# The last two chunks of an output product run block by block, with the routing steps written between them, and the first gathered rows in memory of their own

## The chip, the cores and the metric

The kernel runs on one core of one Trainium2 chip. The time is device microseconds of that core. Its engines are TensorE (PE, with weight loads shown as PEld), VectorE (DVE), ScalarE (ACT), GpSimd (POOL) and the queues that issue transfers (SP's and ACT's above all). TensorE's clock has two levels, 1.2 and 2.4 GHz; the profile gives it as a share of the higher one (0.50 or 1.00).

## The reference, cut to what matters

Two transformer layers on 512 tokens of width 1024, in float32. The change touches the passage from the second mixer to the mixture of experts of the second layer:

```
x = x + merged @ w_out[i]                     # the output product
h = rms_norm_2(x, ffn_norm_g[i])
g_sel = argmax(softmax(h @ w_rg + b_rg))      # one of 4 groups
e_in_group = (h @ w_re + b_re)[g_sel]         # 8 experts of the group
top_p, top_i = top_k(softmax(e_in_group), 2)
for each expert e of 32:                      # gate, up and down matrices
    y += combine[:, e] * (silu(h @ w_gate[e]) * (h @ w_up[e])) @ w_down[e]
x = x + y
```

## The kernel before

All matmuls of the product are made in three parts (`mm3`, lines 249 to 251): each float32 operand is a high and a low half, and high by high, high by low and low by high are summed. A weight chunk of 128x1024 is fetched into a tile `wr` (512 KB, SP's queue, L215), ACT rounds it into `wh` (L203) and DVE takes the rest into `wl` (L206). `c.base` has two `wr` and three pairs `wh`, `wl`.

**The output product.** `merged @ w_out` has four column chunks of 256 (n = 0 to 3), each with two weight chunks (k-blocks 0 to 3 and 4 to 7), so eight weight pairs pass through three pair buffers. Tokens come in four blocks of 128 (t). For n = 0 and 1, `proj_b` runs all blocks of one chunk. For n = 2 and 3, `proj_bt` is written block by block: block t with n = 2, then with n = 3, then `routing.block(t)`. It asks for four pairs at once where there are three; the fourth pair (n = 3, k-blocks 4 to 7) takes the buffer of n = 2's first pair once that is done with all four blocks. Outside of hand-written stretches a scheduler orders each engine's instructions ahead of the run, by program order among those that it takes to be ready, so that the order on the engines is not the written one.

**Routing.** `routing.block(t)`: square of the row `x[t]` with its sum (L1278, ACT), eight transposes of `x[t]` into PSUM in two groups of four (L347) and copies to `hT` (L1283), eight float32 matmuls with the 40 router columns (L1286; the trace has two records for each). `route` and `slots` then work on DVE: inverse root of the mean square (`rsqrt`, L323 to L336), logits (L1298), two rounds of "largest and its index" (L1325 to L1344), then a small matmul that ranks the tokens within each expert (L1349, L1350) and the slot number (L1353 to L1361). Blocks 0 and 1 go together, 2 and 3 singly. `xn` and `hf` hold the scaled rows, whole for blocks 2 and 3 and as halves for 0 and 1. PSUM has four `acc` and four `aux` tiles.

**Experts.** `experts` makes from the slots a one-hot matrix `ohq` for 4 experts x 64 slots (L1378, L1379), and TensorE gathers the tokens' rows by multiplying with it (L1391 with halves, L1388 with the whole rows of blocks 2 and 3). The gathered rows are scaled into `xg` (L1493 DVE, L1491 ACT). Then 16 pairs of experts follow: `up` (L1102), two parts of the next gather, `turn`, `down` (L1122). The order on TensorE in this loop is the written one (`manual_schedule`).

**Expert weights.** 192 chunks of 512 KB (L1077, SP's queue) go through 28 buffers: 15 `wc` of `ring2`, 5 of `ring3`, and the 8 of `c.base`. The first 28 can be fetched before the first expert runs; each later one waits for the release of an earlier one. `ring3` stands where the product's operand `xt` was. `rp` (tag `route`) holds the routing's small tiles, and the pool `exp` (with `xg`, `hid`, `hT`, `ye`) stands partly in its place: the first write to `xg` waits until everything in `rp` has been read, the last reader being the routing weights `wt` (L1434).

Of the kernel before, what the change touches and what calls it, by code (L numbers as in the profile page):

```python
# [9 lines left out]
F32 = mybir.dt.float32  # L10
# [31 lines left out]
RING3 = 5  # L42
# [128 lines left out]
class Chip:  # L171
# [146 lines left out]
    def rsqrt(self, ss, scale, tag="rs", pool=None):  # L318

        v = self.nc.vector  # L320
        sh = list(ss.shape)
        ms = self.sm(sh, F32, tag + "m", pool=pool)
        v.tensor_scalar(ms, ss, scale, EPS, op0=OP.mult, op1=OP.add)  # L323
        y = self.sm(sh, F32, tag + "y", pool=pool)
        t = self.sm(sh, F32, tag + "t", pool=pool)
        v.tensor_scalar(t.bitcast(I32), ms.bitcast(I32), 1, None, op0=OP.logical_shift_right)
        v.tensor_scalar(y.bitcast(I32), t.bitcast(I32), -1.0, float(0x5F3759DF), op0=OP.mult, op1=OP.add)

        for k in (1.0, -2.0, 16.0):
            if sh == [128, 1]:  # L330
                v.scalar_tensor_tensor(t, y, y, ms, op0=OP.mult, op1=OP.mult)
            else:
                v.tensor_tensor(t, y, y, op=OP.mult)
                v.tensor_tensor(t, t, ms, op=OP.mult)
            v.scalar_tensor_tensor(y, t, -3.0 * k * k, y, op0=OP.add, op1=OP.mult)
        v.tensor_scalar(y, y, -1.0 / 8192, None, op0=OP.mult)  # L336
        return y
# [449 lines left out]
def second_mixer(c, x, xt, xtp, xpool, extra):  # L787
# [269 lines left out]
    add_product(c, x, xt, lambda n: a["wout2"][n], routing.block)  # L1057
# [23 lines left out]
class Pair:  # L1081
# [4 lines left out]
    def __init__(self, c, p, chunks, wgu, wdn):  # L1086
# [4 lines left out]
        self.rows = p.tile([64 * self.n, D], F32, name=c.name("ye"), tag="ye", bufs=2)  # L1091
# [82 lines left out]
def more_rounds(c, p, ring, x, hf, rel, wt, iota, wgu, wdn, rounds):  # L1174
# [5 lines left out]
    with tc.For_i(0, rounds * N_EXP * SLOTS, N_EXP * SLOTS) as r:  # L1180
        with tc.For_i(0, N_EXP, 1) as e:
# [23 lines left out]
            ex = Pair(c, p, chunks, [wgu[rows]], [wdn[rows]])  # L1205
# [28 lines left out]
class Routing:  # L1234


    def __init__(self, c, x):
# [20 lines left out]
        self.pl, self.rs, self.xn, self.ss = {}, {}, {}, self.sm([NT], "rss")  # L1258
# [15 lines left out]
    def block(self, t):  # L1274
        c, x, rp = self.c, self.x[t], self.rp
        nc, s = c.nc, c.nc.scalar
        hT = rp.tile([128, KB, 128], F32, name=c.name("hT"), tag="hT", bufs=2)
        s.activation(self.hf[t][:, 0], x, AF.Square, accum_out=self.ss[:, t:t + 1])  # L1278
        for q in range(0, KB, 4):
            ps = c.aux()  # L1280
            for j in range(4):
                c.transpose(ps[:, j * 128:j * 128 + 128], x[:, (q + j) * 128:(q + j + 1) * 128])
            (c.nc.vector.tensor_copy if t == NT - 1 and q else s.copy)(hT[:, q:q + 4], ps.rearrange("p (j t) -> p j t", j=4))  # L1283
        self.pl[t] = c.aux()[:, :40]
        for kb in range(KB):
            nc.tensor.matmul(self.pl[t], hT[:, kb], self.wr[:, kb], start=kb == 0, stop=kb == KB - 1)  # L1286
        if t:
            self.route(range(2) if t == 1 else range(t, t + 1))

        s.dma_start(self.xd[t], x)  # L1290

    def route(self, ts):

        c, v, s = self.c, self.c.nc.vector, self.c.nc.scalar
        tt = slice(ts[0], ts[-1] + 1)
        rs = c.rsqrt(self.ss[:, tt], 1.0 / D, f"rr{ts[0]}", self.rp)
        for i, t in enumerate(ts):
            v.scalar_tensor_tensor(self.lg[:, t].rearrange("p g e -> p (g e)"), self.pl[t], rs[:, i:i + 1], self.rb,  # L1298
                                   op0=OP.mult, op1=OP.add)
        for i, t in enumerate(ts):  # L1300
            self.rs[t] = rs[:, i:i + 1]
            if t < SPLIT:
                self.halve(t)
            else:
                self.xn[t] = self.rp.tile([128, D], F32, name=c.name("xn"), tag="xn", bufs=NT - SPLIT)
                s.activation(self.xn[t], self.x[t], AF.Copy, scale=self.rs[t])
        self.slots(ts)

    def halve(self, t):

        x, h, rs = self.x[t], self.hf[t], self.rs[t]
        self.c.nc.scalar.activation(h[:, 0], x, AF.Copy, scale=rs)
        self.c.nc.vector.scalar_tensor_tensor(h[:, 1], x, rs, h[:, 0].bitcast(F32), op0=OP.mult, op1=OP.subtract)

    def slots(self, ts):

        c, n, tt = self.c, len(ts), slice(ts[0], ts[-1] + 1)
        sm, oh = lambda shape, tag, dt=F32: self.sm([n] + shape, f"{tag}{n}", dt), self.oh[:, :, tt]
        v, pe = c.nc.vector, c.nc.tensor
# [24 lines left out]
        v.tensor_tensor(self.both[:, tt], oh[:, 0], oh[:, 1], op=OP.add)  # L1344

        ps = c.aux()[:, :n * 32].rearrange("p (t e) -> p t e", t=n)
# [4 lines left out]
        tmp = [self.sm([2, n, 32], f"rtmp{k}{n}") for k in range(2)]  # L1351
        ee, rk, ri = (self.sm([2, n], f"{k}{n}", dt) for k, dt in (("ree", F32), ("rrk", F32), ("rri", I32)))
        v.tensor_tensor(tmp[0], oh, eidx[:, None, None, :].to_broadcast([128, 2, n, 32]), op=OP.mult)  # L1353
        v.tensor_reduce(ee, tmp[0], axis=AX.X, op=OP.add)
        v.tensor_tensor(tmp[1], ps[:, None].to_broadcast([128, 2, n, 32]), oh, op=OP.mult)
        v.tensor_reduce(rk, tmp[1], axis=AX.X, op=OP.add)
        v.tensor_copy(ri, rk)
        slot = self.slot[:, :, tt]
        v.scalar_tensor_tensor(slot, ee, float(SLOTS), rk, op0=OP.mult, op1=OP.add)
        v.tensor_scalar(ri, ri, 6, None, op0=OP.logical_shift_right)  # L1360
        v.scalar_tensor_tensor(slot, ri, float((N_EXP - 1) * SLOTS), slot, op0=OP.mult, op1=OP.add)  # L1361


def experts(c, x, routing, xtp, pled, out):
# [34 lines left out]
    for t in range(NT):  # L1399
        eq = onehot(oq, t, slot)  # L1400
# [6 lines left out]

    later = ExitStack()
    later.enter_context(tc.issue_after(eq.ins))
    for t in whole:  # L1410
        routing.halve(t)


    sm, (m1, m2) = routing.sm, routing.m
    pr5 = sm([NT, 5, 8], "pr5")
    v.tensor_tensor(pr5, routing.lg, m1[:, :, :, None].to_broadcast([128, NT, 5, 8]), op=OP.subtract)
    s.activation(pr5, pr5, AF.Exp)
    p1, p2 = sm([NT, 5], "p1"), sm([NT, 5], "p2")
    v.tensor_reduce(p1, pr5, axis=AX.X, op=OP.add)
    v.reciprocal(p1, p1)  # L1420
    v.tensor_tensor(p2, m2, m1, op=OP.subtract)
    s.activation(p2, p2, AF.Exp)
    v.tensor_tensor(p2, p2, p1, op=OP.mult)
    sel, pk = sm([2, NT, 4], "sel"), sm([2, NT], "pk")
    for k, m in enumerate((p1, p2)):
        v.tensor_tensor(sel[:, k], m[:, :, 1:], routing.o[0][:, :, 0, 0:4], op=OP.mult)
    v.tensor_reduce(pk, sel, axis=AX.X, op=OP.add)
    den = sm([NT], "rden")
    v.tensor_tensor(den, pk[:, 0], pk[:, 1], op=OP.add)
    v.reciprocal(den, den)  # L1430
    v.tensor_tensor(den, den, p1[:, :, 0], op=OP.mult)
    wt = c.small.tile([128, 2, NT], F32, name="wt", bufs=1)
    sloti = c.small.tile([128, 2, NT], I32, name="sloti", bufs=1)
    v.tensor_tensor(wt, pk, den[:, None, :].to_broadcast([128, 2, NT]), op=OP.mult)  # L1434
    later.close()

    pc = c.aux()
    for t in range(NT):
        pe.matmul(pc[:, :32], routing.onesb, both[:, t], start=t == 0, stop=t == NT - 1)
    cmax = sm([1], "rcmax")  # L1440
    v.tensor_reduce(cmax, pc[:, :32], axis=AX.X, op=OP.max)
    v.tensor_scalar(cmax, cmax, float(SLOTS - 1), None, op0=OP.add)
    extra = p.tile([128, 2], I32, name="extra")
    v.tensor_copy(extra[:, 0:1], cmax)
    v.tensor_scalar(extra[:, 0:1], extra[:, 0:1], 6, None, op0=OP.logical_shift_right)
    v.tensor_scalar(extra[:, 0:1], extra[:, 0:1], -1, None, op0=OP.add)
    v.tensor_scalar(extra[:, 1:2], extra[:, 0:1], 1, None, op0=OP.min)
    rp.release()
    c.dbg("slot", slot)
    c.dbg("wt", wt)  # L1450

    rows = COMBINED * SLOTS
    ydram = c.dram.tile([rows, D], F32, name="ydram")
    first = c.small.tile([128, 2, NT], F32, name="first", bufs=1)
    v.tensor_scalar(first, slot, float(rows), None, op0=OP.is_lt)
    v.tensor_tensor(first, first, wt, op=OP.mult)
    v.tensor_scalar(sloti, slot, float(rows - 1), None, op0=OP.min)

    ring3 = tc.alloc_tile_pool(name="ring3", bufs=1)
    moe, p = p, tc.alloc_tile_pool(name="exp", bufs=1)  # L1460
# [11 lines left out]
    def xg_tile():  # L1472
        return p.tile([128, KB, 4, 64], F32, name=c.name("xg"), tag="xg", bufs=2)

    def onehots(q):
# [4 lines left out]
        return oq, xg_tile()  # L1480

    def dispatch(oq, xg, kb, ps=None):
# [4 lines left out]
        for j in range(2):  # L1487

            xk, pk, g = xg[:, kb + j], ps[:, j].rearrange("p (e n) -> p e n", e=4), c.col("n_ffn2", kb + j)
            if j:  # L1490
                s.activation(xk, pk, AF.Copy, scale=g)  # L1491
            else:
                v.tensor_scalar(xk, pk, g, None, op0=OP.mult)  # L1493
# [16 lines left out]
    def tail():  # L1510
# [56 lines left out]
        def eat(ps, t, o, n=512, eng=None):  # L1567
            ns = slice(o, o + n)
            tag = "ye" if t % 2 else "xg"
            g = p.tile([128, n], F32, name=c.name("g"), tag=tag, bufs=2)  # L1570
# [53 lines left out]
    cur = oq, xg_tile()  # L1624
    for kb in range(0, KB, 2):
        dispatch(*cur, kb, parts[kb // 2])
    with tc.manual_schedule(engines={mybir.EngineType.PE}):
        for e in range(0, N_EXP, 2):
            q, e4 = divmod(e, 4)
            if e4 == 0 and q < 7:  # L1630
                nxt = onehots(q + 1)
            last = Pair(c, p, chunks, [a["wgu"][e + i] for i in range(2)], [a["wdn"][e + i] for i in range(2)])
# [24 lines left out]
    p.release()  # L1657
    ring3.release()
    op.release()
# [129 lines left out]
```

## Time and profile before

| | |
|---|---|
| median of 3 runs | 1644.61 us (1643.86 to 1648.22) |
| the profiled execution, its own time | 1644.96 us |
| its span, first to last instruction | 1643.0 us |
| TensorE busy | 1543.5 us (94%) |
| VectorE busy | 924.6 us (56%) |
| ScalarE busy | 666.6 us (41%) |
| mean granted clock | 0.98 |
| read from memory | 227.00 MB |

The 1.96 us between the span and the execution's time lie outside the first and last instruction. A busy TensorE is not one at its peak, since its matmuls overlap: one is recorded for 0.28 us where the next starts 0.12 us later.

### The profile page before, as it was taken

To read this page: it belongs to the slowest core of one execution; us is meant where nothing else is said; L and a number is where in the kernel's file an instruction comes from. 1 tells how busy PE (TensorE), PEld (TensorE's weight loads), DVE (VectorE), ACT (ScalarE), POOL (GpSimd) and SP (SyncE) were. 2 spreads that over 40 slices of the span, in tenths; PEclk is the share of its full clock that TensorE was granted. 3 is DMA by queue.
4 is the path that set the end of the run, shared out by engine and by line. 5 is a ranking of instruction groups with operands and counts; after the bars stand their busy time and mean duration, and the time that the engine had idled before them with its cause. 6 is when DMAs were issued, how large, how long until landed. Compare 5 with 4: busy or idle time off the path is not lost.

```text
span 1643.0 us, 24293 instructions
## 1 busy us (share of the span) xinstructions
PE 1543.5 (94%) x9602; PEld 1266.7 (77%) x9602; DVE 924.6 (56%) x2109; ACT 666.6 (41%) x1098; POOL 109.3 (7%) x80
## 2 busy tenths in 40 slices
PE   6979899999999999999999997999998899999867
PEld 6757889899899888988899987977888645544356
DVE  4569688878846764265636228777543523221274
ACT  4455546766723543144423334598122211101043
POOL 1052310000000000000000003000000000000042
PEclk9999999999999999999999998999999899999979
DMA  4432122223333322243324332212248499999951
GB/s 158 144 102 84 59 78 78 73 71 115 106 101 116 116 87 71 74 144 100 87 93 167 104 103 90 91 39 90 68 164 295 172 378 371 377 371 379 373 223 54
DMA packets 75466, 244.99 MB, mean 149 GB/s; under 512 B 7728, under 2 KB 16688, under 8 KB 75216
## 3 DMA queue, kind: packets, MB, share of 16 engines
q1 hardware_dynamic: 69152, 220.80, 39.4%
q10 hardware_dynamic: 4464, 16.25, 2.5%
q0 software_dynamic: 1728, 6.29, 1.0%
q8 instruction: 79, 1.29, 0.3%
q14 instruction: 43, 0.35, 0.1%
HBM read 227.00 MB, written 16.32 MB: 148 GB/s over the span
## 4 chain that ended last, share of the span: by engine, by line
PE 67%; DVE 14%; DMA 8%; ACT 6%; issue 3%; POOL 1%; SPq 0%; ACTq 0%; DVEq 0%; POOLq 0%
PE acc L249 16%; PE acc L250 16%; PE acc L251 16%; DMA wc<-in_wgu_dram 5%; PE acc L1102 4%; PE aux L347 3%; PE acc L1122 2%; PE aux L1391 2%; DVE wl L206 2%; ACT wh L203 1%; PE aux L627 1%; DMA ydram<-ye 1%; DVE de L547 1%; ACT pb L604 1%; DVE xn L355 1%
## 5 line engine op out<-in xcount | busy, mean ns | idle before, releaser
L206 DVE TENSOR_TENSOR wl<-wr,wh 128x1024 fp32r<-128x1024 f32 (+1 forms) x178 | 214.8, 1209 | 254.0 <-ACT wh L203 245.5
L203 ACT ACTIVATE wh<-wr 128x1024 fp32r<-128x1024 f32 (+1 forms) x182 | 189.5, 1046 | 318.1 <-PE acc L251 165.6
L250 PE MATMUL acc<-xtl,wh 128*128 128x512 f32 (+2 forms) x744 | 278.7, 375 | 0.0
L249 PE MATMUL acc<-xth,wh 128*128 128x512 f32 (+2 forms) x744 | 277.4, 373 | 1.3 <-ACT wh L203 1.2
L251 PE MATMUL acc<-xth,wl 128*128 128x512 f32 (+2 forms) x744 | 276.8, 372 | 0.0
L249 PE MATMUL acc<-wh,xth 128*128 128x256 f32 x928 | 262.9, 284 | 3.3 <-ACT z L408 1.8
L250 PE MATMUL acc<-wl,xth 128*128 128x256 f32 x928 | 262.4, 283 | 3.2 <-DVE wl L206 1.8
L251 PE MATMUL acc<-wh,xtl 128*128 128x256 f32 x928 | 263.7, 285 | 0.8 <-DVE xtl L206 0.8
L249 PEld LDWEIGHTS acc<-wh,xth 128*128 128x128 f32 x928 | 176.0, 190 | 7.9 <-ACT z L408 3.5
L250 PEld LDWEIGHTS acc<-wl,xth 128*128 128x128 f32 x928 | 176.2, 190 | 5.3 <-DVE wl L206 3.0
L251 PEld LDWEIGHTS acc<-wh,xtl 128*128 128x128 f32 x928 | 176.3, 190 | 1.9 <-DVE xtl L206 1.0
L249 PEld LDWEIGHTS acc<-xth,wh 128*128 128x128 f32 (+1 forms) x744 | 139.4, 187 | 27.2 <-ACT wh L203 1.9
L251 PEld LDWEIGHTS acc<-xth,wl 128*128 128x128 f32 (+1 forms) x744 | 139.3, 187 | 25.2 <-issue 0.5
L250 PEld LDWEIGHTS acc<-xtl,wh 128*128 128x128 f32 (+1 forms) x744 | 139.3, 187 | 24.1 <-issue 0.5
L1102 PE MATMUL acc<-wc,xg 128*64 128x512 f32 x512 | 130.5, 609 | 11.6 <-DMA wc<-in_wgu_dram 6.4
L1102 PEld LDWEIGHTS acc<-wc,xg 128*64 128x64 f32 x512 | 40.7, 139 | 98.2 <-issue 65.3
L249 PE MATMUL acc<-wh,acth 128*128 128x256 f32 x352 | 98.7, 280 | 0.1
L251 PE MATMUL acc<-wh,actl 128*128 128x256 f32 x352 | 98.3, 280 | 0.0
L250 PE MATMUL acc<-wl,acth 128*128 128x256 f32 x352 | 98.2, 279 | 0.0
L1106 DVE TENSOR_TENSOR hid<-hid,acc 128x256 f32<-128x256 f32 x16 | 6.7, 421 | 116.4 <-ACT hid L1105 116.3
L249 PEld LDWEIGHTS acc<-wh,acth 128*128 128x128 f32 x352 | 66.5, 189 | 0.6 <-ACT acth L203 0.5
L761 DVE SCALAR_TENSOR_TENSOR fcv<-acc,cols,fcv 128x511 f32<-128x511 f32 x88 | 65.7, 747 | 1.5
(452 smaller groups left out, 2636.4 us busy)
## 6 DMA issues: line engine op xcount, KB each, us to landing
wc<-in_wgu_dram SPq DMA_DIRECT2D x128, 512.0 KB, 9.3
wc<-in_wdn_dram SPq DMA_DIRECT2D x64, 512.0 KB, 10.1
wr<-in_wup_dram SPq DMA_DIRECT2D x44, 512.0 KB, 3.6
wr<-in_w2a_dram SPq DMA_DIRECT2D x28, 512.0 KB, 3.5
wr<-in_wqkv_dram SPq DMA_DIRECT2D x24, 512.0 KB, 3.7
wr<-in_wout_dram SPq DMA_DIRECT2D x24, 512.0 KB, 3.8
wr<-in_wdown_dram SPq DMA_DIRECT2D x16, 512.0 KB, 3.5
ydram<-ye ACTq DMA_DIRECT2D x15, 512.0 KB, 7.4
```

The lines of the kernel that those rows point to most:

```text
L203: nc.scalar.activation(hi, src, AF.Copy)
L206: (nc.vector if engines[1] == "v" else nc.gpsimd).tensor_tensor(lo, src, hi.bitcast(F32), op=OP.subtract)
L249: mm(out, a[0], b[0], start=start, stop=False)
L250: mm(out, a[0], b[1], start=False, stop=False)
L251: mm(out, a[1], b[0], start=False, stop=stop)
L347: self.nc.tensor.transpose(out, src, self.ident[:rows, :rows])
L355: nc.vector.scalar_tensor_tensor(out, xt_, r, wrow, op0=OP.mult, op1=OP.mult)
L547: v.tensor_scalar(de[:, h], ab[:, h], at[:, h:h + 1], 0.0, op0=OP.subtract, op1=OP.min)
L761: v.scalar_tensor_tensor(y[:, sh:], ps[:, :T - sh], cv(k), y[:, sh:], op0=OP.mult, op1=OP.add)
L1102: c.nc.tensor.matmul(ps[self.half(i)], xg(kb, i), self.wu[kb // 2][i][:, kb % 2 * 512:kb % 2 * 512 + 512], start=kb == 0, stop=kb == KB - 1)
L1122: c.nc.tensor.matmul(ps[n][self.half(i)], self.hT[:, j, self.half(i)], self.wd[j][i][:, n * 512:n * 512 + 512], start=j == 0, stop=j == 1)
L1391: pe.matmul(ps[:, j], hf[t][:, k, ks], oq[:, t], start=start and k == 0, stop=stop and k == 1)
```

## The change

1. `add_product` is gone from this place. n = 0 and 1 run as before; n = 2 and 3 are run by the new `Routing.last`, in which the order of TensorE and ACT is the written one. The fourth weight pair has two buffers of its own, two of `ring2`'s 15 `wc` (`split_chunk`).
2. The routing is cut into `turn` (four transposes and their copy), `square` (half a row), `logits`, `choose` (inverse root, logits, largest), `rank` (rank within the expert, slot) and `scale` (`xn`, `hf`), set by hand between the products. `rsqrt` adds the sums of the two half rows with one more instruction. All four copies of a block are ACT's now (before, the last one was DVE's).
3. The writes of `x` to memory for the overflow path (`x3d`, 4 x 512 KB on ACT's queue) come after the whole of it.
4. `experts` moves the routing weights (`wt`), the second halves of blocks 2 and 3, the count for the overflow and the next one-hot matrix behind the first gather's copies (`issue_after(taken.ins)`, DVE's order alone). Of the copies into `xg`, every second group of two is DVE's and every other ACT's.
5. `xg` of even quarters, `hid` and `hT` stand in a pool `exp0` of their own that needs no memory of `rp`; `ye`, `xg` of odd quarters and the rest stay in `exp`, behind `rp`. To make room `ring3` has 3 buffers instead of 5, and a `ring4` with 2 comes after the release of `rp`: 26 buffers ahead of that, 28 behind it.

```diff
-RING3 = 5
+RING3 = 3
+RING4 = 2
     routing = Routing(c, x)
-    add_product(c, x, xt, lambda n: a["wout2"][n], routing.block)
+    for n in range(2):
+        c.proj_b(xt, a["wout2"][n], residual(c, x, n))
+    routing.last(xt, [a["wout2"][n] for n in (2, 3)])
...
+        def product(t, i, kbs=range(KB)):
+            if t % 2 == 0 and kbs[0] == 0:
+                acc[i] = c.acc().rearrange("p (a b) -> p a b", a=2)
+            for kb in kbs:
+                w, o = ws[i][kb // 4], kb % 4 * 256
+                c.mm3(acc[i][:, t % 2], tuple(h[:, kb, t * 128:t * 128 + 128] for h in xt),
+                      (w[0][:, o:o + 256], w[1][:, o:o + 256]), kb == 0, kb == KB - 1)
+            if kbs[-1] == KB - 1:
+                o = x[t][:, 512 + i * 256:768 + i * 256]
+                self.added = v.tensor_tensor(o, acc[i][:, t % 2], o, op=OP.add)
+
+        first, rest = range(4), range(4, KB)
+        with self.c.tc.manual_schedule(engines={mybir.EngineType.PE, mybir.EngineType.Activation}):
+            product(0, 0)
+            turn(0, 0)
+            square(0, 0)
+            product(0, 1)
+            turn(1, 0)
+            square(1, 0)
+            product(1, 0)
+            turn(0, 4)
+            square(0, 1)
+            product(1, 1)
+            logits(0)
+            turn(2, 0)
+            square(2, 0)
+            product(2, 0)
+            turn(1, 4)
+            square(1, 1)
+            product(2, 1, first)
+            logits(1)
+            self.choose((0, 1))
+            turn(3, 0)
+            square(3, 0)
+            product(2, 1, rest)
+            self.scale(0)
+            self.scale(1)
+            product(3, 0)
+            turn(2, 4)
+            square(2, 1)
+            product(3, 1, first)
+            logits(2)
+            self.choose((2,))
+            self.scale(2)
+            logits(3, first)
+            product(3, 1, rest)
+            self.rank((0, 1))
+            square(3, 1)
+            turn(3, 4)
+            logits(3, rest)
+            self.choose((3,))
+            self.scale(3)
+            self.rank((2,))
+            self.rank((3,))
+        for t in range(NT):
+            s.dma_start(self.xd[t], x[t])
+
+    def split_chunk(self, c, src, beside):
+        if not beside:
+            return c.weights(src)
+        h, l = (self.ring.tile([128, 1024], F32R, name=c.name("wc"), tag="wc", bufs=RING2) for _ in "hl")
+        c.split(h, l, c.fetch(src))
+        return h, l
...
+    cur, taken = (oq, xg_tile(0)), None
     for kb in range(0, KB, 2):
-        dispatch(*cur, kb, parts[kb // 2])
+        taken = dispatch(*cur, kb, parts[kb // 2]) or taken
+    later = ExitStack()
+    later.enter_context(tc.issue_after(taken.ins))
...
+    nxt = onehots(1)
+    later.close()
+    rp.release()
+    p = tc.alloc_tile_pool(name="exp", bufs=1)
+    ring4 = tc.alloc_tile_pool(name="ring4", bufs=1)
+    chunks.add(ring4, "wc", RING4)
```

## Rows read from the trace of the kernel before

**Rows 1.** Windows: length, busy time by engine, granted clock, DMA share, GB/s

```profile
1238.00:1268.00 30.00, 28.84 (x233) 27.20 (x232) 9.13 (x30) 8.16 (x14) 0.00 (x0) 1.00 0.81 279
1250.00:1255.00 5.00, 5.00 (x42) 4.82 (x42) 0.65 (x2) 1.06 (x1) 0.00 (x0) 1.00 0.85 342
1288.00:1305.00 17.00, 11.74 (x46) 7.47 (x48) 12.14 (x54) 3.30 (x7) 0.00 (x0) 0.85 0.01 1
1414.00:1535.00 121.00, 114.64 (x563) 54.18 (x562) 27.23 (x64) 13.14 (x27) 0.00 (x0) 1.00 1.00 376
```

**Rows 2.** Chain that ended last, 1285 us to the end: start, length, what

```profile
1299.53 0.41 DVE xg L1493
...
1300.57 10.05 PE acc L1102 x32
...
1318.40 6.87 PE acc L1102 x32
```

**Rows 3.** Timeline of SP's queue: start, length, what was issued

```profile
1238.28 0.33 SPq L215 DMA_DIRECT2D wr<-in_wout_dram  x1
...
1304.27 0.80 SPq L1077 DMA_DIRECT2D wc<-in_wgu_dram  x2
```

**Rows 4.** All transfers from 1305 to 1536 us

```profile
DMA packets 23628, 86.20 MB, mean 373 GB/s; under 512 B 2616, under 2 KB 2616, under 8 KB 23616
```

**Rows 5.** The same chain in the product: the last weight chunks

```profile
1235.93 1.07 ACT wh L203
1237.03 1.24 DVE wl L206
1238.28 6.55 DMA wr<-in_wout_dram
```

**Rows 6.** Timeline of TensorE: start, length, what [idle before, ended by]

```profile
1241.47 0.82 PE L347 MATMUL aux<-cst,x 128*128 128x128 f32 x6
1242.05 0.36 PE L249 MATMUL acc<-wh,xth 128*128 128x256 f32 x1
...
1247.34 1.05 PE L1286 MATMUL aux<-wr,hT 128*128 128x40 f32 x8
1248.21 0.36 PE L250 MATMUL acc<-wl,xth 128*128 128x256 f32 x1
...
1273.68 0.21 PE L1350 MATMUL aux<-rboth,strib 128*128 128x32 bf16 x1 [5.74 <-DVE rboth L1344]
...
1289.10 6.29 PE L1388 MATMUL acc<-ohq,xn 128*128 128x256 f32 x28
```

**Rows 7.** Timeline of TensorE: two earlier gaps of the second mixer

```profile
993.66 0.45 PE L347 MATMUL aux<-cst,ryn 128*128 128x128 f32 x1 [4.17 <-DVE ryn L875]
...
1013.39 0.48 PE L347 MATMUL aux<-cst,ryn 128*128 128x128 f32 x1 [4.94 <-DVE ryn L875]
```

**Rows 8.** Windows of 1 us on TensorE: length, busy, granted clock, DMA, GB/s

```profile
999.00:1000.00 1.00, 1.00 (x9) 0.81 0.00 0
...
1016.00:1017.00 1.00, 1.00 (x9) 0.78 0.56 66
```

**Rows 9.** Timeline of VectorE from the product to the first expert

```profile
1239.97 0.42 DVE L710 TENSOR_TENSOR x<-acc,x 128x256 f32<-128x256 f32 x1
...
1264.04 0.17 DVE L323 TENSOR_SCALAR rr0m<-rss 128x2 f32<-128x2 f32 x1
...
1266.62 0.43 DVE L1298 SCALAR_TENSOR_TENSOR lg<-aux,rr0y,rb 128x40 f32<-128x40 f32 x2
...
1284.78 0.26 DVE L1298 SCALAR_TENSOR_TENSOR lg<-aux,rr3y,rb 128x40 f32<-128x40 f32 x1 [1.71 <-PE aux L1286]
...
1290.85 0.48 DVE L1379 SCALAR_TENSOR_TENSOR ohq<-cst,slot,oht 128x256 fp32r<-128x256 f32 x1
...
1298.89 0.17 DVE L1434 TENSOR_TENSOR wt<-pk,rden 128x8 f32<-128x8 f32 x1
```

**Rows 10.** Timeline of ScalarE: the square of a whole row

```profile
1258.11 1.06 ACT L1278 ACTIVATE hf<-x 128x1024 fp32r<-128x1024 f32 x1 [3.37 <-DVE x L710]
```

## The forecast, on record ahead of the run

> **What bounds the kernel now.** I read the windows by stage first, then the chain that ended last, then the timelines of single engines where the chain changes hands. Two stages matter. From 1414 to 1535 us the transfers are busy all the time (share 1.00) while TensorE has 6 us of gaps [rows 1]: the experts wait for their weights. Over 1305 to 1536 us 86.20 MB come at 373 GB/s [rows 4], so a chunk of 524,288 bytes takes 1.41 us. Ahead of that, from 1288 to 1305 us, the transfers stand still (share 0.01) [rows 1]: all 28 buffers are full and SP's next chunk goes out only at 1304.27 [rows 3], when the first expert's matmuls have released one. Since the transfers are the bound from there to the last experts, the end of the kernel moves with the moment at which they resume, and with the number of chunks still to come then. Nothing else of the passage counts for the time.
>
> What sets that moment is a serial passage. The product's last matmul ends at 1273.68 - 5.74 = 1267.94 [rows 6]. TensorE then waits 5.74 us for the choice of blocks 0 and 1, turns blocks 2 and 3 at the lower clock, and the last gather ends at 1289.10 + 6.29 = 1295.4 [rows 6]. The first `xg` copy starts at 1299.53, just behind `wt` at 1298.89 [rows 2, 9], although its data were there 4 us earlier: it waits for the memory of `rp`. The first expert starts at 1300.57 and takes 10.05 us where the second takes 6.87 [rows 2], because the clock fell meanwhile.
>
> **The late weight pair.** With the order written by hand, TensorE goes from product(0,0) to four transposes, to product(0,1). Its k-blocks 4 to 7 need the eighth weight pair. The fetch of that can't start before 1238.28, since it needs the `wr` that the sixth pair's split on DVE frees at 1237.03 + 1.24 [rows 3, 5]; nothing in the change moves that. It takes 6.55 us, behind the expert chunks that SP issued before, and ACT and DVE add 1.07 and 1.24 [rows 5]: ready at about 1247.2. TensorE has product(0,0) behind it at 1239.97 [rows 9]. A matmul of the product costs 5.00/42 = 0.119 us [rows 1], a transpose (1242.05 - 1241.47)/6 = 0.097, a record of the logits (1248.21 - 1247.34)/8 = 0.109 [rows 6]. So 4 transposes and 12 matmuls end at 1241.9 (factor 1.07, next paragraph), and TensorE stands for 5.3 us. Before, it had the other blocks to go on with. Queued behind it are all later products and turns, so this is paid in full.
>
> **The product with the turns in it.** Before, from 1239.97 to 1267.94, TensorE made 168 matmuls (20.0 us), 16 transposes (1.6) and 32 records of logits (3.5): 25.1 us in 28.0, of which 1.1 were idle (28.84 busy of 30.00) [rows 1], so a factor of 1.07 for changes between them. After, the same stretch holds 168 matmuls, 28 transposes (2.7) and 56 records (6.1): 28.8 x 1.07 = 30.8 us, 28.9 of them behind the wait. The product ends at 1247.2 + 28.9 = 1276.1 at full clock.
>
> **The clock in that gap.** No row shows this very gap. The two nearest, of 4.17 and 4.94 us [rows 7], were both followed by the lower level until inside the windows at 999 and 1016 us, whose means are 0.81 and 0.78 [rows 8]: from a half to a whole these put the return at 999.4 and 1016.4, 5.7 and 3.1 us after TensorE resumed. Half of that is lost: 2.9 and 1.5. The bounds are 0 and 2.9; I take the mean of the two, 2.2, since my gap is a little longer than both but broken by one matmul at 1246. The product ends at 1278.3, which is 10.4 us later than before.
>
> **From there to the first expert.** DVE's sum 0.6 with its hand-over, a half square 0.8 (half of 1.06 and the read of the sum) [rows 10], the inverse root 2.8 (2.58 from 1264.04 to 1266.62 for 13 instructions, now 14) and 0.7, an estimate, for sharing DVE with the ranks and one-hots of blocks 0 to 2. From a block's logits on DVE to the end of its one-hot it took 1291.33 - 1284.78 = 6.5 [rows 9]. Its gather is 16 records at 6.29/28 = 0.225: 3.6 us [rows 6]. Together 15.0 us, against 27.5 before (1267.94 to 1295.4). TensorE's own path (3 us to the last logits, 3.8 for the gathers of blocks 0 and 1, 32 records as dense as the product's, 7.2 for 2 and 3) is 14.0, so the two are near each other. The first expert starts at 1293.3: with `xg` in memory of its own the copies run beside the last gather, and the 5.2 us gap goes. No fall of the clock comes with it, so the first buffer is free not 3.70 but 1.85 us after that start [rows 2, 3]: 1295.2.
>
> **The sum.** The transfers resume 1304.27 - 1295.2 = 9.1 us sooner. As `ring4` comes only with the release of `rp`, 26 chunks are there by then and not 28: 2 x 1.41 = 2.8 us of transfers come back. 9.1 - 2.8 = 6.3 us. From the profiled execution's own 1644.96 us, which stands 0.35 above the median of the runs, that is 1638.7 us.
>
> **Edits at no cost.** The additional instructions of `rsqrt` for blocks 0 to 2, the half squares and ACT's fourth copy run beside the products (ACT is busy 8.2 of 30 us there) [rows 1]. The other split of copies between DVE and ACT in the expert loop hides behind transfers. If that cover were gone, each late copy would cost its 0.4 us in 28 places. `wt`, the halves and the next one-hot, now behind the copies, hide under the first expert's 6.87 us [rows 2] and about 1 to 2 us more, in which TensorE waits but the transfers don't: eight buffers are free by then and take 11 us to fill. What waits behind `rp` is the first `ye` and the odd `xg`, both needed later than that.
>
> The `x3d` writes move to the end of the written stretch, on ACT's queue. They are 2.10 MB, 5.6 us at the rate of [rows 4]. They are hidden if they go out while TensorE still works on the routing, when the buffers are full; uncovered they cost 5.6 us. The Trainium skill (DMA: Bandwidth & Descriptors, section Issuing engines are not separate DMA queues) says that transfers begun by different engines run on the same 16 DMA engines and interleave, so ACT's queue would be no cover by itself. The trace shows both queues at work but no such collision at 1288 to 1305 us, where the share is 0.01 [rows 1]; by the page alone the sum would be 6.3 - 5.6 = 0.7 us. I take the cover, with that as a rival.
>
> **Rivals.**
> A. The clock doesn't fall in the gap, or the eighth pair comes a few us sooner because fewer chunks are ahead of it. For it: the gap is broken by a matmul. Against: both near gaps fell. Gain 6.3 + 2.2 = 8.5 (1636.5), and 2.8 more with two chunks fewer ahead of the fetch: 1633.7. Chance 0.24.
> B. The other side: SP issues in order, and the two fetches into `ring4` stand in its queue ahead of those that reuse freed buffers. Then the transfers resume only with the release of `rp`. From the last one-hot to the end of `wt` that took 1299.06 - 1291.33 = 7.7 us [rows 9], and now some one-hot instructions can come between, 1.5 us by their 0.3 to 0.5 each: 1293.3 + 9.2 = 1302.5, a gain of 1.8, less 2.8: 1.0 slower, 1646.0. It decides against the change from 8.2 us on. For it: program order. Against: the scheduler orders SP by what it takes to be ready, and the buffers free up first. Chance 0.14.
> C. The half clock comes again at the end, where logits and transposes leave TensorE thinly used, and the gathers run on it: 1.5 to 2.9 us more, 1640.9. For it: blocks 2 and 3 were turned at half clock before. Against: the gaps are under 1 us. Chance 0.12.
> D. The `x3d` writes meet the resuming chunks: 1644.3. Chance 0.05.
>
> The forecast itself (5.3 us of waiting, half clock after it) has 0.43, with 1636.8 to 1640.3 as its own range; 0.02 is left for what I don't see.
>
> **How the numbers follow.** About 0.3%, 4.9 us, is what a measurement of this kernel can tell from no change, so faster means under about 1639.7. The forecast case is there by 0.37 of its 0.43, A with all of its 0.24, C with 0.01: 0.62. Slower than that bound are only the far end of B (a release some 14 us late) and the unseen: 0.07. The same: 0.31. The range reaches from A's far end, 1633, to B's 1646 and holds all but some 0.15.
>
> **What the profile will show.** Right: a gap on TensorE of about 5 us that ends near 1247 with a release by DVE's `wl`; the granted clock at 0.50 after it; the last product matmul near 1278; L1102 starting at about 1293 with no gap ahead of it, lasting 7 and not 10 us; SP's next chunk at about 1295; from 1300 on every expert some 6 us earlier. Wrong: SP idle between 1295 and 1302 (B), no fall near 1247 (A), the gathers at 0.45 us a record (C), or a late eighth pair: each us there is a us at the end.

## The result and the profile after

The changed kernel takes 1630.94 us in the median of 4 runs (1625.99 to 1633.76), the kernel before 1646.41 us beside it (1643.86 to 1652.15): a ratio of 0.9898, 95% interval 0.9861 to 0.9935. Two later comparisons of the same pair gave 0.9921 (0.9902 to 0.9940) and 0.9906 (0.9884 to 0.9929). Over all 16 runs the median is 1631.46 us, over the 42 of before in the experiments' comparisons 1645.46: 14.0 us faster. The forecast was 1638.7 with a range down to 1633.0; the change gains more than twice the 6.3 us that it was given.

The profiled execution took 1630.64 us, its span is 1628.9 us. Its passage starts 1.00 us later than in the profile of before: SP fetches `x` at 1218.19 instead of 1217.19, and issues the eighth weight pair's fetch at 1239.28 instead of 1238.28 [rows 3, 5]. The windows of the changed kernel (length, busy time of each engine, granted clock, DMA share, GB/s):

```profile
core 0: us, PE busy (x) PEld busy (x) DVE busy (x) ACT busy (x) POOL busy (x), PEclk, DMA share, GB/s
1218.00:1241.00 23.00, 23.00 (x204) 23.00 (x203) 10.94 (x24) 4.88 (x5) 0.00 (x0) 1.00 0.45 147
1238.00:1268.00 30.00, 27.68 (x240) 27.29 (x240) 13.29 (x38) 12.33 (x24) 0.00 (x0) 1.00 0.90 332
1245.00:1250.00 5.00, 4.56 (x39) 4.56 (x39) 0.98 (x3) 1.21 (x3) 0.00 (x0) 1.00 0.95 326
1288.00:1305.00 17.00, 17.00 (x94) 8.23 (x96) 10.18 (x40) 5.66 (x10) 0.00 (x0) 1.00 0.82 298
```

From 1288 to 1305 us, where the transfers stood still before [rows 1], their share is 0.82 and TensorE has no gap. The clock is 1.00 in every one of these windows: in this passage it never fell. What is new is the first row: from 1218 to 1241 us, still under the earlier products, the transfers are less than half busy. SP's queue tells why:

```profile
1228.40 11.21 SPq L216 DMA_DIRECT2D wr<-in_wout_dram  x3
1241.08 9.44 SPq L1085 DMA_DIRECT2D wc<-in_wgu_dram  x9
1251.93 6.04 SPq L1085 DMA_DIRECT2D wc<-in_wdn_dram  x4
...
1289.84 2.52 SPq L1085 DMA_DIRECT2D wc<-in_wgu_dram  x4
1293.27 0.33 SPq L1085 DMA_DIRECT2D wc<-in_wdn_dram  x1
1295.92 0.80 SPq L1085 DMA_DIRECT2D wc<-in_wgu_dram  x2
```

No expert chunk goes out ahead of the eighth weight pair; the first one is issued at 1241.08. So the transfers stand still when the pair's fetch is issued, where before they were busy all the time. From 1235 to 1240 us, first the kernel before, then the changed one:

```profile
1235.00:1240.00 5.00, 5.00 (x45) 4.84 (x43) 2.97 (x5) 2.12 (x2) 0.00 (x0) 1.00 1.04 386
1235.00:1240.00 5.00, 5.00 (x47) 5.00 (x46) 1.97 (x4) 2.13 (x2) 0.00 (x0) 1.00 0.00 0
```

In SP's queue, the four of 1289.84 are the first that reuse a buffer (before: 1304.27 [rows 3]), and `ring4`'s two come after them, at 1295.92. The chain that ended last, from that pair to the first expert (start, length, what):

```profile
1238.03 1.24 DVE wl L207
1239.28 3.77 DMA wr<-in_wout_dram
1243.08 1.06 ACT wc L204
1244.16 1.23 DVE wc L207
...
1272.60 0.42 DVE x L1316
...
1276.09 1.19 PE acc L1473 x8
...
1283.62 0.49 DVE ohq L1461
1284.12 0.14 issue
1284.26 3.69 PE acc L1470 x16
1287.95 7.02 PE acc L1110 x32
```

The fetch takes 3.77 us where it took 6.55 [rows 5]. The last sum of the product is at 1272.60, the last gather takes 3.69 us and the first expert follows it at once, in 7.02 us instead of 10.05 [rows 2]. TensorE's own timeline has the wait in two parts, 1.45 + 0.88 = 2.33 us:

```profile
1242.46 0.28 PE L252 MATMUL acc<-wh,xtl 128*128 128x256 f32 x1
1244.18 0.38 PE L250 MATMUL acc<-wc,xth 128*128 128x256 f32 x1 [1.45 <-ACT wc L204]
1245.44 0.38 PE L251 MATMUL acc<-wc,xth 128*128 128x256 f32 x1 [0.88 <-DVE wc L207]
```

### The profile page after: what moved, and what is told of

The parts are those of the page before. It is cut to its first block, busy times and chain, and to the rows that moved or that the text cites. A ratio compares the mean times of both kernels' runs of the same rounds, so it can differ in the third digit from the quotient of the medians.

```text
span 1628.9 us, 24318 instructions
## 1 busy us (share of the span) xinstructions
PE 1536.5 (94%) x9602; PEld 1261.6 (77%) x9602; DVE 923.6 (57%) x2111; ACT 666.5 (41%) x1107; POOL 109.4 (7%) x80
## 4 chain that ended last, share of the span: by engine, by line
PE 70%; DVE 13%; DMA 6%; ACT 6%; issue 3%; POOL 1%; SPq 0%; ACTq 0%; DVEq 0%; POOLq 0%
PE acc L250 17%; PE acc L251 16%; PE acc L252 16%; PE acc L1110 5%; DMA wc<-in_wgu_dram 4%; PE aux L353 3%; PE aux L1473 3%; PE acc L1130 2%; DVE wl L207 2%; ACT wh L204 1%; PE aux L633 1%; DVE de L553 1%; DVE rst L337 1%; ACT pb L610 1%; DVE xn L361 1%
## 5 line engine op out<-in xcount | busy, mean ns | idle before, releaser
L207 DVE TENSOR_TENSOR wl<-wr,wh 128x1024 fp32r<-128x1024 f32 (+1 forms) x177 | 213.5, 1209 | 250.2 <-ACT wh L204 245.4
L250 PE MATMUL acc<-wh,xth 128*128 128x256 f32 x912 | 258.5, 284 | 2.7 <-ACT z L414 1.6
L251 PE MATMUL acc<-wl,xth 128*128 128x256 f32 x912 | 257.9, 283 | 2.0 <-DVE wl L207 1.3
L252 PE MATMUL acc<-wh,xtl 128*128 128x256 f32 x912 | 259.0, 285 | 0.8 <-DVE xtl L207 0.8
L251 PEld LDWEIGHTS acc<-wl,acth 128*128 128x128 f32 x352 | 66.5, 189 | 0.1
```

What stands on the lines that cost most here:

```text
L207: (nc.vector if engines[1] == "v" else nc.gpsimd).tensor_tensor(lo, src, hi.bitcast(F32), op=OP.subtract)
L250: mm(out, a[0], b[0], start=start, stop=False)
L251: mm(out, a[0], b[1], start=False, stop=False)
L252: mm(out, a[1], b[0], start=False, stop=stop)
```

## The experiments

Each ratio is to runs of the kernel before on the same chip. "Resume" is SP's first fetch into a reused buffer, "stage" the time from there to the last expert's silu, the last `hid` row on ACT.

**1. The expert chunks ahead of the eighth pair again.** Its high and low parts get a tag of their own, so that the chunks need not come behind it in the turns of the tag `wc`:

```diff
-RING2 = 15
+RING2 = 13
-        h, l = (self.ring.tile([128, 1024], F32R, name=c.name("wc"), tag="wc", bufs=RING2) for _ in "hl")
+        h, l = (self.ring.tile([128, 1024], F32R, name=c.name("wc"), tag="w8", bufs=2) for _ in "hl")
...
     chunks.add(routing.ring, "wc", RING2)
+    chunks.rings[9:9] = [(routing.ring, "w8", 2)] * 2
```

> The changed kernel, but the high and low parts of the eighth weight pair have two tiles of a tag of their own (taken from ring2's fifteen, and given to the chunks at places 9 and 10), so that SP's order of fetches becomes the one of the kernel before: eight expert chunks ahead of the eighth pair's fetch. Theory (the forecast failed because the change let that fetch go out without chunks ahead of it): the eighth pair is ready at about 1247 to 1248 again, TensorE stands some 5 us after product(0,0) instead of 2.3, and the first expert starts 2.8 us later at full clock (about 1290.7, some 1633.7 us in all) or 5.0 us later if the clock falls in that gap as forecast (about 1292.9, some 1636). Rival (the place of that fetch has nothing to do with it; chunks that come earlier help as much as the pair suffers): the same time as the changed kernel, 1630.9, gap still about 2.3 us.

Measured: 1637.16 us (ratio 0.9951, 0.9933 to 0.9969). SP's queue of this kernel, then its chain, TensorE's timeline, the last sum of the product on DVE, and the windows:

```profile
1220.36 1.30 SPq L1085 DMA_DIRECT2D wc<-in_wgu_dram  x3
1228.20 2.12 SPq L216 DMA_DIRECT2D wr<-in_wout_dram  x2
1230.38 3.50 SPq L1085 DMA_DIRECT2D wc<-in_wgu_dram  x5
1239.08 0.33 SPq L216 DMA_DIRECT2D wr<-in_wout_dram  x1
```

```profile
1239.08 6.05 DMA wr<-in_wout_dram
...
1247.95 0.21 PE acc L252
1248.16 0.21 PE acc L250
```

```profile
1246.26 0.38 PE L250 MATMUL acc<-wc,xth 128*128 128x256 f32 x1 [3.71 <-ACT wc L204]
1247.51 0.44 PE L251 MATMUL acc<-wc,xth 128*128 128x256 f32 x1 [0.88 <-DVE wc L207]
```

```profile
1276.14 0.42 DVE L1316 TENSOR_TENSOR x<-acc,x 128x256 f32<-128x256 f32 x1 [0.94 <-PE acc L252]
```

```profile
1245.00:1250.00 5.00, 2.87 (x13) 2.67 (x14) 1.22 (x1) 1.06 (x1) 0.00 (x0) 0.77 0.99 355
1250.00:1255.00 5.00, 5.00 (x41) 5.00 (x40) 1.02 (x3) 1.92 (x5) 0.00 (x0) 0.89 0.88 356
```

With eight chunks issued ahead of it the fetch takes 6.05 us. Four of the eight are still under way when it goes out and land ahead of it, the last at 1243.88 us; the pair's own lands 1.24 us later, the pace at which the chunks land, and those issued right behind it come after it. So it waits for what is ahead, not for what follows. The gap is 3.71 + 0.88 = 4.6 us, and the clock falls: matmuls start 0.21 us apart instead of 0.12, the windows' means are 0.77 and 0.89. This is the case that the forecast described, and the rival falls. In size it is near the theory's second branch: the first silu comes 3.7 us later than in the changed kernel, not 5.0, and the time is 1637.2, not 1636. The gain on the kernel before is 8.4 us, where the forecast had 6.3.

**2. The same again, beside the changed kernel.**

> The eight expert chunks ahead of the eighth weight pair's fetch once more, now beside the changed kernel. Theory: 3.7 us slower than the changed kernel, as the first expert came in the first profile (2.3 us of gap, 1.5 of clock). Rival (the 6 us between the two comparisons were more than scatter, the early chunks do harm of their own): 6 us or more slower.

Measured: 1637.79 us over 12 runs (0.9956, 0.9941 to 0.9970), against 1631.24 for the changed kernel beside it: 6.5 us, the rival's number and not the theory's 3.7. In this profile the clock fell a second time, in the gathers:

```profile
1280.00:1285.00 5.00, 4.33 (x27) 4.17 (x27) 4.53 (x33) 2.50 (x3) 0.00 (x0) 0.58 0.91 299
1285.00:1290.00 5.00, 5.00 (x29) 4.69 (x27) 2.52 (x14) 0.25 (x1) 0.00 (x0) 0.73 1.03 419
```

From the last sum of the product to the first silu took 25.2 us here, 22.4 in the changed kernel and in the first profile of experiment 1. Up to the first silu, counted from SP's fetch of `x`, this profile is 7.3 us behind the changed kernel: 2.3 for the late pair, 2.2 for the clock behind it, 2.8 for the fall in the gathers. The profile of experiment 1 is only 3.7 us behind there, and still its run took 6.0 us longer (1636.64 against 1630.64); the rest is in its stage, 253.1 us against 250.2, which is within what experiment 6 shows for one and the same program. So the late pair and the clock behind it account for 3.7 to 4.5 of some 6 us. Whether the other 2 are falls of the clock in the gathers or harm of another kind, as the rival says, isn't shown, and why the gathers are hit in one profile and not in the other is open.

**3. The experts' half alone**: the product and routing of before, the pools, copies and rings of the change.

> Only the second half of the change: the xg buffers in a pool of their own, copies of the first gathered rows ahead of the weights and halves, ring3 of 3 and ring4 of 2 behind the release of rp; the product and the routing steps as in the kernel before. Theory (the end moves with the moment at which the chunks resume, and each chunk not fetched early costs 1.41 us): the gap of 5.2 us ahead of the first expert goes, its matmuls run at full clock, SP's next chunk goes out at about 1298 instead of 1304.3; 6.3 less 2.8 = 3.5 us faster than before, about 1642.9 with before at 1646.4. Rival 1 (two chunks fewer cost nothing): 6.3 us faster, 1640.1. Rival 2 (SP held by ring4's fetches until rp is released): no gain, 1646 to 1647.

Measured: 1641.63 us (0.9967, 0.9951 to 0.9982), 3.9 us less than the 1645.58 of before beside it. TensorE and SP in its profile:

```profile
1299.12 7.09 PE L1103 MATMUL acc<-wc,xg 128*64 128x512 f32 x32
```

```profile
1301.08 2.52 SPq L1078 DMA_DIRECT2D wc<-in_wgu_dram  x4
```

The first expert follows the last gather with no gap, at full clock. SP resumes at 1301.08 in a profile whose passage starts 3.1 us later than that of before (`x` at 1220.26), so 6.3 us sooner, as the theory has it; less two chunks its 3.5 us hold. Rival 2, SP held by `ring4`, falls here as in the changed kernel. Rival 1, that two chunks fewer cost nothing (6.3 us faster), lies within the interval; experiment 7 prices the chunks.

**4. The product's half alone**: `Routing.last`, with the pools and the order of the experts of before.

> Only the first half of the change: the last two chunks of the product by token block with the routing steps set between them; pools and order of the experts as in the kernel before (28 chunks early, xg in the memory of rp). Theory: the product ends near 1272.6 as in the changed kernel, the last gather near 1287 to 1288, then the wait for the release of rp of 3 to 4 us and a first expert at the lower clock; SP resumes at about 1296, 8 to 9 us sooner than before and with no chunk lost: about 1638. Rival (the two halves only pay together, since the weights and halves that come first take the place of the time won): less than 4 us faster than before, over 1642.

Measured: 1636.63 us (0.9951, 0.9935 to 0.9967), 9.0 us less than before. SP resumes 8.3 us sooner than before, counted from its fetch of `x`, and the theory (about 1638) holds; the rival, less than 4 us, falls. The gap and the lower clock ahead of the first expert are still there:

```profile
1289.01 9.84 PE L1109 MATMUL acc<-wc,xg 128*64 128x512 f32 x32 [5.34 <-ACT xg L1572]
```

The halves give 3.9 and 9.0, together 12.9 us, against 14.0 for the change: within the scatter they add, and the product's half is over two thirds of it.

**5. The eighth pair fetched early**, into a third tile, ahead of the chunks:

```diff
-RING2 = 15
+RING2 = 12
...
-        h, l = (self.ring.tile([128, 1024], F32R, name=c.name("wc"), tag="wc", bufs=RING2) for _ in "hl")
-        c.split(h, l, c.fetch(src))
+        h, l, raw = (self.ring.tile([128, 1024], dt, name=c.name("wc"), tag="w8", bufs=3) for dt in (F32R, F32R, F32))
+        c.nc.sync.dma_start(raw, src)
+        c.split(h, l, raw)
...
+    chunks.rings[9:9] = [(routing.ring, "w8", 3)] * 3
```

> The changed kernel, but the eighth weight pair is fetched into a third tile of its own, so that it need not wait for the buffer that the sixth pair's split frees; two expert chunks, then the sixth and seventh pair, then six more chunks follow on SP. Theory (serial passage): the eighth pair is ready before product(0,0) ends, the gap of 2.3 us on TensorE goes, the whole passage and the end come 2.3 us sooner: about 1628.6. Rival (the passage is bound by the choice on DVE or by the transfers that fill the buffers, not by TensorE's gap): the same as the changed kernel, 1630.9 within 0.1%.

Measured: 1630.34 us (0.9916, 0.9890 to 0.9943), no different from the changed kernel within the scatter of its runs (1625.41 to 1639.96). In the profile TensorE has no gap (10.00 of 10 us busy from 1240 to 1250) and the first silu comes 74.0 us after SP's fetch of `x`, against 76.9; the stage then takes 252.9 instead of 250.2 us. Inconclusive by itself; experiment 7 has the early pair once more.

**6. The changed kernel again**, twice.

> The changed kernel itself once more, beside the next three, since the two halves and the variants so far differ by less than its runs scatter. Theory (the changed kernel gains by the 14.4 us by which its chunks resume sooner, less 2.8 for two chunks not there, 11.6): a ratio to before of 0.993. Rival (its two halves pay more together than one after the other; or what the first comparison showed is the rule): a ratio of 0.990 as in the first comparison, 0.988 to 0.991.

> The changed kernel a third time, as the base for the three kernels beside it. Theory (the gain is the 14 to 15 us by which the chunks resume sooner less 2.8, and the 3.2 us between the first two comparisons are the scatter of the transfer rate in the experts' stage): 1631 to 1635 us. Whether the clock falls in the gap of 2.3 us on TensorE seems to be open in each execution: if it does, the first expert comes 1.5 us later.

Measured: 1633.82 us (0.9921), between the theory's 0.993 and the rival's 0.988 to 0.991, so that it decides nothing, and 1631.24 us (0.9906), within the 1631 to 1635 expected. Up to the resume the three profiles agree within 0.2 us, counted from SP's fetch of `x`; behind it they don't. The windows of the stage, and the last silu, first of the changed kernel's first profile and then of the second:

```profile
1310.00:1530.00 220.00, 209.17 (x1077) 100.79 (x1077) 56.09 (x140) 23.74 (x53) 0.00 (x0) 0.99 0.99 381
```

```profile
1540.05 0.38 ACT L1113 ACTIVATE hid<-acc 128x256 f32<-128x256 f32 x1 [7.10 <-PE acc L1110]
```

```profile
1310.00:1530.00 220.00, 206.51 (x1064) 99.13 (x1062) 54.62 (x136) 23.71 (x52) 0.00 (x0) 0.99 0.98 374
```

```profile
1544.97 0.38 ACT L1113 ACTIVATE hid<-acc 128x256 f32<-128x256 f32 x1 [7.21 <-PE acc L1110]
```

The same program moves 381 and 374 GB/s here: 220 us x 7 GB/s = 1.5 MB, three chunks, worth 4 us. The stages are 250.2, 255.6 and (third profile) 250.3 us. A difference of a few us between two single profiles says nothing about this stage; only medians do. The granted clock scatters with it: in each of these kernels the longer runs tend to have the lower mean clock (of the first four of the changed kernel 0.985 in that of 1625.99 us, 0.982 in that of 1633.76). Which of the two brings the other isn't shown.

**7. 24 and 28 early chunks, and both mends together.** 24: `RING3 = 1`, `RING4 = 4`. 28: `hT` in a pool released after the last rank, whose memory then holds `ring3`'s other two buffers:

```diff
-RING3 = 3
-RING4 = 2
+RING3 = 5
+RING4 = 0
+        hp = self.c.tc.alloc_tile_pool(name="turns", bufs=1, side="right")
-                hT[t] = self.rp.tile([128, KB, 128], F32, name=c.name("hT"), tag="hT", bufs=2)
+                hT[t] = hp.tile([128, KB, 128], F32, name=c.name("hT"), tag="hT", bufs=2)
...
             self.rank((3,))
+        hp.release()
...
-    chunks.add(ring4, "wc", RING4)
```

> The changed kernel with one buffer in ring3 and four in ring4: 24 chunks instead of 26 can be there before the first expert, the total of 28 and all else unchanged. Theory (each chunk not fetched before the first expert is 1.41 us of transfers later): 2.8 us slower than the changed kernel in the same comparison; the span from SP's first reused chunk to the last expert's silu grows from about 251 to about 254 us. Rival (the early chunks have slack, the term of 2.8 us in the forecast was no cost): the same time as the changed kernel within 0.5 us.

> The changed kernel with the turned blocks hT in a pool that is released after the last rank, so that ring3 has all five buffers before the first expert again and ring4 none: 28 chunks early. Theory (1.41 us a chunk): 2.8 us faster than the changed kernel in the same comparison, and 249 to 250 us from SP's first reused chunk to the last silu. Rival (the last buffers can't be filled in time, since the fetches between 1241 and 1290 us are already dense, with the four x3d writes among them): less than 1 us faster.

> Both mends of the changed kernel: the eighth weight pair in a third tile of its own, fetched ahead of the chunks, and 28 chunks early. Theory (the two terms add): 2.3 + 2.8 = 5.1 us faster than the changed kernel in the same comparison; no gap on TensorE after product(0,0), SP's first reused chunk about 2.5 to 3 us sooner, 249 to 250 us from there to the last silu. Rival (the end is set by the sum of all transfers from the first chunk on, so that an earlier first expert is given back): no faster than with the 28 chunks alone.

Measured, beside 1633.82 for the changed kernel: 1635.09 us with 24 (0.9936, 0.9921 to 0.9951), 1630.26 with 28 (0.9904, 0.9888 to 0.9920), 1626.65 with 28 and the early pair (0.9890, 0.9871 to 0.9908). The kernels with 24 and with 28 are alike up to the first silu (78.4 and 78.5 us after the fetch of `x`), so they price a chunk: (1635.09 - 1630.26)/4 = 1.2 us. Their runs don't overlap (1634.47 and up, 1633.28 and down). Each alone can't be told from its rival, since the changed kernel's six runs beside them reach from 1628.11 to 1636.11; but the two rivals together would allow 1.5 us between 24 and 28 chunks, not 4.8, so together they fall. The stages agree: 249.1 to 250.6 us in the four profiles with 28 chunks (mean 249.7), 250.1 to 255.6 in eight with 26, the one with the late writes of experiment 8 left out (251.8), 253.6 with 24. The two mends add to 7.2 us beside the changed kernel and to 4.8 against the median of all its 16 runs, so the theory's 5.1 is borne out within the scatter. Against 28 chunks alone the early pair brings 3.6 us, and the first silu 4.5 us sooner (in the profile with 28 alone the clock fell, see below); the rival has no difference there. The runs of the two overlap (four of the six lie below the other's lowest), so this is likely rather than shown. The kernel with both has the lowest median of all.

The clock shows something else. The gap on TensorE in the kernels with 24 and with 28 is the changed kernel's (1.45 + 0.88 and 1.50 + 0.88), and still it fell. With 24:

```profile
1245.00:1250.00 5.00, 5.00 (x30) 5.00 (x31) 0.59 (x2) 1.21 (x3) 0.00 (x0) 0.66 0.98 339
```

Eight profiles have this gap of 2.1 to 2.4 us (the changed kernel three times, experiments 4, 7 twice, and 8 twice): in four the clock stayed at 1.00, in four it fell to 0.66 to 0.72 in the window behind it, and the product ended 1.5 to 2.2 us later.

**8. The `x3d` writes** behind the fifth pair's silu, and left out.

> The changed kernel with the four x3d writes (2.10 MB on ACT's queue) moved from the end of the routing into the experts' stage, behind the silu of the fifth pair. Theory (the experts' stage is bound by the 16 DMA engines, and the writes share them with the chunks whichever queue starts them): about 5.6 us slower than the changed kernel beside it. Rival (ACT's queue is a way of its own, or the stage has room): the same within 1 us.

> The changed kernel without the four x3d writes (left out; only the path for overfull experts reads them). Theory (forecast's rival D is no cost here: the buffers are full at about 1285 us, before SP's first reused chunk at 1289.8, so the writes delay nothing that counts): the same as the changed kernel beside it within 1 us. Rival (the fetches between 1241 and 1290 us are the bound, and the writes cost their 5.6 us): up to 5.6 us faster.

Measured, beside 1631.24 for the changed kernel: 1633.69 us late (0.9925, 0.9900 to 0.9949), 1633.24 without them (0.9928, 0.9905 to 0.9952). Leaving work out can't cost 2 us by itself; in its profile the clock fell in the gap and again in the gathers, and all three intervals overlap. Inconclusive for the price of late writes: neither the theory's 5.6 us nor nothing. That leaving them out gains less than the rival's 5.6 us is clear, so nothing shows that they set the end where they stand. The Trainium skill (DMA: Bandwidth & Descriptors, section Issuing engines are not separate DMA queues) has transfers of all issuing engines interleave on the same 16; the late writes landed within 4.5 us (median) while chunks that took about 10 were under way on SP's queue, so that much agrees; the price that would follow, the 5.6 us, isn't shown.

## Why the prediction was wrong

**The step that failed** is in the late weight pair: "It takes 6.55 us, behind the expert chunks that SP issued before". That was read from the kernel before and carried over. The moment of issue, of which the forecast says "nothing in the change moves that", was right (1238.28, and 1239.28 less the 1.00). But the change does move the chunks: the pair takes two tiles of the tag `wc`, and the chunks that share the tag come behind it. The fetch took 3.77 us, and the gap was 2.33 us, not 5.3. Experiment 1 gives the pair a tag of its own; eight chunks go ahead of it again, and fetch and gap grow to 6.05 and 4.6 us. That kernel takes 1637.2 and 1637.8 us, near the 1638.7 of the forecast, though partly by luck: in its two profiles the transfers resume 2.6 us sooner and 0.9 us later than forecast, counted from the fetch of `x`.

The transfers resumed 6.4 us sooner than forecast: 2.8 by the pair, 2.2 by the clock that followed from it, 1.7 by the product, less 0.4 behind it. Rival A named the first two ("the eighth pair comes a few us sooner because fewer chunks are ahead of it"), with 0.24 and 1633.7; it had two chunks fewer in mind, and there were none. Without the product's 1.7 the range ended at 1633, above the measured time.

The terms, with the profile's times less 1.00 us:

| step | forecast | profile after |
|---|---|---|
| last part of the eighth pair ready | 1247.2 | 1244.4 |
| clock in the gap | 2.2 lost | 0 |
| product behind the wait | 28.9 | 27.2 |
| product ends | 1278.3 | 1271.6 |
| to the first expert | 15.0 | 15.4 |
| to the first free buffer | 1.85 | 1.89 |
| chunks resume | 1295.2 | 1288.8 |
| two chunks fewer | 2.8 given back | 2.4, from experiment 7 |

**The clock** followed from the gap, but not strictly. With the long gap (4.6 and 3.6 us) it fell in both profiles, and cost 28.63 - 27.16 = 1.5 us in the first (1247.51 to 1276.14 for the product, against 1245.44 to 1272.60) and 2.2 in the second, so the forecast's 2.2 was of the right size. With the short one it fell in four profiles of eight: that it stayed up in the three of the changed kernel is partly luck.

**The product** was mis-sized: the factor of 1.07 for changes between products, turns and logits should have been 27.2/27.0 (28.8 less the 1.8 for what ran ahead of the wait), about 1.0. The hand-written order leaves no gaps on TensorE behind the wait: it is busy all the time from 1250 to 1270 us.

**What held:** the 15.0 us from the product's end to the first expert, with no gap ahead of it and no half clock; the first buffer free about 1.85 us later; `ring4` behind the reused buffers (rival B did not come); the price of a chunk (1.41 against 1.2). So 1304.27 - 1288.84 = 15.4 us sooner, less 2.4 is 13.0, against 14.0 in the medians. The 1.0 left is within the scatter that experiment 6 shows. Rival C, half clock in the gathers, is absent from the changed kernel's three profiles and present in two of its variants (experiments 2 and 8). Rival D did not come in that size: leaving the `x3d` writes out gains nothing that can be seen.

## What to carry to other kernels

When a change gives a tile another tag or pool, follow the whole queue of that tag: whatever shares it is ordered behind, and a fetch with idle DMA engines ahead of it can be much shorter than one behind chunks (3.77 against 5.45 to 6.55 us here). A mend that moves an urgent fetch ahead of prefetches is worth trying by itself; the fastest kernel here has the pair first, the chunks right behind it, and all 28 of them early. And where a stage is bound by transfers, compare medians and the moment at which it starts, not the ends of two profiles.

## What the runs showed of the hardware

The same gap of 2.1 to 2.4 us on TensorE left the clock at 2.4 GHz in four profiles and took it to 1.2 GHz for a while in four others, at 1.5 to 2.2 us each. The Trainium skill (TensorE: Matmul & The Clock Gate, Part 1: The HAM clock gate) says that the chip watches TensorE's activity in windows that run free of the program; by that rule the same gap can fall to either side, and four against four fits that, but no run shows that this is the reason. And one program's transfers moved 374 to 381 GB/s over the same 220 us, which is worth 4 us of its time.
